# Attention scores: the pass over the keys' low part is cut to the 64 rows that hold the queries' high part, with two heads on the two row halves of TensorE

## The chip, the cores and the metric

The kernel runs on one core of a Trainium2 chip. The metric is the device time of one execution in microseconds, of which several runs are made; one execution was also taken by the hardware profiler, and all rows below come from that one. In the rows PE is TensorE's matmul, PEld its weight load, DVE is VectorE, ACT is ScalarE, POOL is GpSimd, SP is SyncE.

## The reference

Two layers of a diffusion backbone, over 128 context tokens and 512 latent tokens (five token tiles of 128). A layer has one input projection, a state-space branch, two attention branches with 8 heads of 64 (2 key heads, each shared by 4 query heads), a gated merge, and an MLP of width 4096. What the change touches is the score product of the two attention branches:

```
def _blocked_attention(q, k, v, sink):
...
        s = jnp.einsum('bqhgd,bkhd->bhgqk', qq, k).astype(jnp.float32) * ATTN_SCALE
...
        p = jax.nn.softmax(s, axis=-1)[..., :n_k]
        return jnp.einsum('bhgqk,bkhd->bqhgd', p.astype(v.dtype), v)
```

The windowed branch does the same over the key tiles within 128 positions, the 128 cached context keys and a sink logit; the global branch sees all 512 latent keys and the 128 cached ones. The context tile sees itself only.

## The kernel before

Every fp32 product is split: an operand is written as a high part (rounded to the shorter matmul type) and a low part (what is left), and a product is made of three passes (high by high, low by high, high by low) that accumulate in one PSUM bank.

The scores do this in two passes. `queries` (line 863) writes for each of the 8 heads a stationary operand `qs[:, hd]` of 128 rows by 128 queries. The 64 rows of a head's high part lie in the lower half (rows 0 to 63) for even heads and in the upper half (rows 64 to 127) for odd heads, and the low part is in the other half. `keys` (line 837) writes `KH` and `KL`, the keys' high and low part, each **twice**, in both row halves. So one pass of `KH` over 128 rows adds high by high and low by high at once (line 915), and one pass of `KL` adds high by low and low by low (line 916).

`attend` (line 876) takes one token tile: for each of 2 key heads `v` and 2 pairs of query heads `pr` it writes the scores of the pair into two banks `pp[0]` and `pp[1]` (tag `sc`, three such banks in all), one bank for each head. The key blocks are grouped into `runs` of neighbours, one matmul of 128 to 512 columns for each run. In the windowed branch (`i == 0`) a pass with `maskb` (line 920) adds the band's mask. In the global branch (`i == 1`) the last two key blocks go to a third bank `p5` (lines 923 to 925). Then VectorE takes the maxima (line 926), ScalarE the exponentials (line 938), TensorE transposes them (line 947), they are split (line 950) and multiplied with the values (lines 954 and 955).

The pair-of-heads loop runs 4 times in a token tile, 5 token tiles, 2 branches and 2 layers: 80 pairs, 160 heads. Attention is not alone on TensorE: the order in which each engine's instructions stand is made at build time by a scheduler with a timeline model, which places matmuls of the projections and gates (lines 159 to 161 and 170 to 172) between those of attention. Each engine then runs its instructions in that order, and waits on semaphores.

Some matmuls of the kernel use only part of TensorE's columns: the transposes of the keys by `ident` (line 855: 64 columns, two column halves) and the conditioning product (lines 187 and 524: 32 columns, four column groups). No matmul of the kernel before uses only part of the rows.

Of the kernel before, what the change touches and what calls it, by code (L numbers as in the profile page):

```python
# [30 lines left out]
def net(tc, I, O, depth=DEPTH, dbg=None):  # L31
    nc = tc.nc
    V, S, G, T, SY = nc.vector, nc.scalar, nc.gpsimd, nc.tensor, nc.sync
# [26 lines left out]
    def psc():  # L60
        return bank("sc", 3)

    def ppt():
        return bank("pt", 2)

    def ppv():
        return bank("pv", 1)
# [17 lines left out]
    identb = base.tile([128, 128], BF, name="identb")  # L85
    V.tensor_copy(identb, ident)
    maskb = base.tile([128, 384], BF, name="maskb")
# [29 lines left out]
    def split(hi, lo, src, half=False):  # L117

        if half:
            S.activation(hi, src, AF.Copy, scale=0.5)  # L120
            V.scalar_tensor_tensor(lo, src, 0.5, hi, op0=ALU.mult, op1=ALU.subtract)
        else:
            S.activation(hi, src, AF.Copy)  # L123
            V.tensor_tensor(lo, src, hi, op=ALU.subtract)  # L124
# [368 lines left out]
    def phase_a(l, h):  # L493
# [113 lines left out]
        for ft in range(4):  # L607
            ws = wtile(I["w_u"][l, ft], 8) if ft >= len(uacc) else None
            us = uall[:, ft]
            for c in (0, 17, 83):  # L610
                n = 2 if c == 17 else 1
                G.memset(us[:, :, c:c + n], 0.0)
            for i, (t0, t1) in enumerate(SPLITS):
                n = (t1 - t0) * 128
# [3 lines left out]
                v = p[:, :n].rearrange("p (c j) -> p j c", j=8)  # L618
# [257 lines left out]
        def attend(i, t, qs, KH, KL, VV, y):  # L876

            if t == 0:
                blks = (0,)
            elif i == 0:  # L880
                blks = tuple(b for b in (t - 1, t, t + 1) if 1 <= b <= 4) + (5,)
            else:
                blks = (1, 2, 3, 4, 5)

            runs = []
            n1 = 4 if len(blks) < 5 else 3
            for b in blks[:n1]:
                if runs and runs[-1][-1] == b - 1:
                    runs[-1].append(b)
                else:  # L890
                    runs.append([b])
            nb = len(blks)
            order = blks
            stat = atp[0].tile([128, 4, 8], F32, name="stat", tag="stat", bufs=2)
            ng, sm, sx, rs = (stat[:, j] for j in range(4))
            for v in range(2):
                po = ppv()
                for pr in range(2):
                    h0 = 4 * v + 2 * pr
                    hs = slice(h0, h0 + 2)  # L900
                    part = atp[0].tile([128, 2, 2], F32, name="part", tag="part", bufs=4)

                    pp = [psc(), psc()]
                    p5 = psc() if nb > 4 else None
                    n4 = 128 * min(nb, n1)
                    Ps = [atp[0].tile([128, 640 if i else 512], F32, name="P", tag="P", bufs=4) for _ in range(2)]
                    for z_ in range(2):
                        hd = h0 + z_
                        o = 0
                        for r in runs:  # L910
                            n = 128 * len(r)
                            c0 = 128 * r[0]
                            oo = pp[z_][:, o:o + n]
                            msk = i == 0 and t > 0 and r[0] < 5
                            T.matmul(oo, qs[:, hd], KH[:, v, c0:c0 + n], start=True, stop=False)
                            T.matmul(oo, qs[:, hd], KL[:, v, c0:c0 + n], start=False, stop=not msk)
                            if msk:
                                nm = 128 * sum(b < 5 for b in r)
                                m0 = 128 * (r[0] - t + 1)
                                T.matmul(oo[:, 0:nm], identb, maskb[:, m0:m0 + nm], start=False, stop=True)  # L920
                            o += n
                        if p5 is not None:
                            o5 = p5[:, 256 * z_:256 * z_ + 256]
                            T.matmul(o5, qs[:, hd], KH[:, v, 512:768], start=True, stop=False)
                            T.matmul(o5, qs[:, hd], KL[:, v, 512:768], start=False, stop=True)
                        V.reduce_max(part[:, 0, z_:z_ + 1], pp[z_][:, 0:n4], axis=AX.X, negate=True)
                    n0 = part[:, 0]
                    if i == 0:
                        V.tensor_tensor(ng[:, hs], n0, nsink[:, 1, hs], op=ALU.min)
                    else:  # L930
                        if p5 is not None:
                            V.reduce_max(part[:, 1], p5.rearrange("p (z n) -> p z n", z=2), axis=AX.X, negate=True)
                            V.tensor_tensor(n0, n0, part[:, 1], op=ALU.min)
                        V.tensor_tensor(ng[:, hs], n0, ssq[:, t, hs], op=ALU.mult)  # L934
                    for z_ in range(2):
                        oh = slice(h0 + z_, h0 + z_ + 1)
                        sc_ = ssq[:, t, oh] if i else 1.0
                        S.activation(Ps[z_][:, 0:n4], pp[z_][:, 0:n4], AF.Exp, scale=sc_, bias=ng[:, oh], accum_out=sm[:, oh])
                        if p5 is not None:
                            S.activation(Ps[z_][:, 384:640], p5[:, 256 * z_:256 * z_ + 256], AF.Exp, scale=sc_, bias=ng[:, oh], accum_out=sx[:, oh])  # L940
                    for z0 in range(0, nb, 2):
                        zs = range(z0, min(z0 + 2, nb))
                        n = 256 * len(zs)
                        p = ppt()
                        for z in zs:
                            for z_ in range(2):
                                T.transpose(p[:, (2 * (z - z0) + z_) * 128:(2 * (z - z0) + z_ + 1) * 128], Ps[z_][:, z * 128:(z + 1) * 128], ident)
                        ph = atp[0].tile([128, 512], F32R, name="ph", tag="ph", bufs=3)
                        pl = atp[0].tile([128, 512], F32R, name="pl", tag="pl", bufs=2)
                        split(ph[:, 0:n], pl[:, 0:n], p[:, 0:n])  # L950
                        for z in zs:
                            zc = slice(256 * (z - z0), 256 * (z - z0) + 256)
                            oo = po[:, 256 * pr:256 * pr + 256]
                            T.matmul(oo, VV[:, order[z], v], ph[:, zc], start=(z == 0), stop=False)
                            T.matmul(oo, VV[:, order[z], v], pl[:, zc], start=False, stop=(z == nb - 1))

                pz = po.rearrange("p (r z n) -> p r z n", r=2, z=2)
                yv = y[:, t, 2 * v:2 * v + 2]
                yt = atp[0].tile([128, 2, 128], F32, name="yt", tag="yt", bufs=2 if i else 1)
                S.activation(yt[0:64], pz[64:128, :, 0], AF.Copy)  # L960
                S.activation(yt[64:128], pz[0:64, :, 1], AF.Copy)
                V.tensor_tensor(yv[0:64], pz[0:64, :, 0], yt[0:64], op=ALU.add)
                V.tensor_tensor(yv[64:128], pz[64:128, :, 1], yt[64:128], op=ALU.add)
            if nb > 4:
                V.tensor_tensor(sm, sm, sx, op=ALU.add)
            if i == 0:
                V.tensor_tensor(sx, nsink[:, 0], ng, op=ALU.add)
                S.activation(sx, sx, AF.Exp)
                V.tensor_tensor(sm, sm, sx, op=ALU.add)
            V.reciprocal(rs, sm)  # L970

            rx = atp[0].tile([128, 640 if i else 512], F32, name="P", tag="P", bufs=4)[:, 0:512].rearrange("p (a b) -> p a b", a=8)
            S.activation(rx, rs.unsqueeze(2).to_broadcast([128, 8, 64]), AF.Copy)
            p = ppt()
            for j in range(4):
                T.transpose(p[:, j * 128:(j + 1) * 128], rx[:, 2 * j:2 * j + 2].rearrange("p a b -> p (a b)"), ident)
            V.tensor_tensor(y[:, t], y[:, t], p.rearrange("p (j n) -> p j n", j=4), op=ALU.mult)
# [8 lines left out]
        def attend_all(i, K, y):  # L986
            qs = qtile(i, 0)
            for t in range(NT):
                nxt = qtile(i, t + 1) if t + 1 < NT else None
                attend(i, t, qs, *K, y)  # L990
                qs = nxt
# [18 lines left out]
        for b in range(8):  # L1010
# [9 lines left out]
            for q in range(4):  # L1020
                o = p[:, q * NCH:(q + 1) * NCH]
# [100 lines left out]
        for i2 in range(2):  # L1122
            ws = wtile(I["w_glu"][l, i2], 4)
            for f in range(2):
                ft = 2 * i2 + f
                sg = t640("sg")
                for t0, t1 in SPLITS:
                    p = pg()
                    n = (t1 - t0) * 128
# [360 lines left out]
```

## Time and profile before

| | before |
|---|---|
| median of 3 runs | 2401.14 us (2400.68 to 2404.61) |
| the profiled execution | 2402.64 us |
| its span, first to last instruction | 2400.8 us |
| mean granted TensorE clock | 0.977 |
| PE busy / weight load busy | 95% / 86% of the span |
| DVE / ACT / POOL busy | 62% / 41% / 23% |

The profiled execution's own time lies 1.8 us around its span, and 1.5 us above the median. A matmul's row shows its start and a modelled length; matmuls overlap, so the pace of TensorE is read from one start to the next, not from the length. The form `128*64` in a row means 128 rows and 64 columns of TensorE, `128x384` that 384 columns stream.

### The profile page before, as it was taken

The page shows a single profiled execution, that of the slowest core. Times are in us where ns is not written, and L with a number is a line of the kernel's source. Part 1 is how long each engine was busy: PE and PEld are TensorE (multiplying, and loading weights), DVE is VectorE, ACT ScalarE, POOL GpSimd, SP SyncE. Part 2 cuts the span into 40 slices and gives each one's busy share as a digit, 9 for nine tenths or more (in the row PEclk, how much of TensorE's full clock was granted, in tenths as well). Part 3 has the DMA queues.
Part 4 walks back from the last instruction along what each step waited for, and adds up shares of the span by engine and source line. Part 5 has one row for each costly group of instructions (what it writes and reads, how often), then busy time and mean ns, then how long its engine had stood idle before and what let it go on. Part 6 is the DMA issues. An engine that isn't in the chain of part 4 may idle for free. (4 is left out here: it accounts for less than half of the span.)

```text
span 2400.8 us, 38820 instructions
## 1 busy us (share of the span) xinstructions
PE 2287.4 (95%) x14904; PEld 2072.1 (86%) x14904; DVE 1481.5 (62%) x3001; ACT 990.9 (41%) x2316; POOL 556.6 (23%) x615
## 2 busy tenths in 40 slices
PE   7887999999999999999998889999999889999997
PEld 4777897799997988888888889999999789998885
DVE  7887854766348956663665766466743873444457
ACT  2324655565344432222234256566642353332221
POOL 2555700001024311100531661000102550000046
PEclk8998999999999999999999999999999999999999
DMA  7423236722232345556335313522222422222221
GB/s 271 138 82 106 94 114 210 237 79 83 80 132 75 117 152 172 172 166 201 125 105 148 116 60 118 156 68 72 72 74 68 175 80 79 73 78 77 74 80 53
DMA packets 126361, 277.93 MB, mean 116 GB/s; under 512 B 40640, under 2 KB 60224, under 8 KB 126176
## 3 DMA queue, kind: packets, MB, share of 16 engines
q1 hardware_dynamic: 126176, 275.45, 35.2%
q8 instruction: 117, 1.92, 0.3%
q14 instruction: 68, 0.56, 0.1%
HBM read 240.97 MB, written 38.63 MB: 116 GB/s over the span
## 5 line engine op out<-in xcount | busy, mean ns | idle before, releaser
L124 DVE TENSOR_TENSOR wlo<-raw,whi 128x512 fp32r<-128x512 f32 x472 | 361.3, 773 | 296.1 <-ACT whi L123 288.9
L123 ACT ACTIVATE whi<-raw 128x512 fp32r<-128x512 f32 x472 | 292.6, 631 | 437.7 <-PE p_sc L1206 144.5
L159 PE MATMUL p_g<-hh,whi 128*128 128x256 f32 (+1 forms) x1224 | 384.5, 315 | 4.0 <-ACT hh L123 3.1
L161 PE MATMUL p_g<-hh,wlo 128*128 128x256 f32 (+1 forms) x1224 | 383.0, 314 | 3.5 <-DVE wlo L124 3.3
L160 PE MATMUL p_g<-hl,whi 128*128 128x256 f32 (+1 forms) x1224 | 382.7, 313 | 3.3 <-DVE hl L124 3.3
L159 PEld LDWEIGHTS p_g<-hh,whi 128*128 128x128 f32 x1224 | 234.0, 191 | 11.8 <-ACT hh L123 3.9
L161 PEld LDWEIGHTS p_g<-hh,wlo 128*128 128x128 f32 x1224 | 234.1, 191 | 5.6 <-DVE wlo L124 5.0
L160 PEld LDWEIGHTS p_g<-hl,whi 128*128 128x128 f32 x1224 | 234.4, 191 | 4.6 <-DVE hl L124 4.0
L159 PE MATMUL p_sc<-hh,whi 128*128 128x256 f32 (+1 forms) x648 | 203.2, 315 | 4.8 <-ACT hh L123 4.5
L160 PE MATMUL p_sc<-hl,whi 128*128 128x256 f32 (+1 forms) x648 | 203.3, 314 | 4.0 <-DVE hl L124 4.0
L161 PE MATMUL p_sc<-hh,wlo 128*128 128x256 f32 (+1 forms) x648 | 202.7, 313 | 0.1
L1090 POOL TENSOR_TENSOR mt<-sg,mt 128x640 f32<-128x640 f32 x24 | 40.5, 1686 | 647.5 <-DVE stat L934 276.4
L170 PE MATMUL p_g<-whi,hh 128*128 128x256 f32 x480 | 143.1, 301 | 10.0 <-DVE rt L785 6.2
L171 PE MATMUL p_g<-wlo,hh 128*128 128x256 f32 x480 | 142.3, 297 | 3.9 <-DVE wlo L124 3.4
L159 PE MATMUL p_g<-act,whi 128*128 128x384 f32 x448 | 141.3, 315 | 4.7 <-ACT mtmp L192 3.0
L124 DVE TENSOR_TENSOR pl<-p_pt,ph 128x512 fp32r<-128x512 f32 (+1 forms) x176 | 102.9, 591 | 64.0 <-ACT ph L123 54.1
L1290 DVE TENSOR_TENSOR rl<-rl 128x384 f32<-128x384 f32 (+1 forms) x128 | 75.9, 594 | 106.3 <-ACT rl L1289 106.3
L172 PE MATMUL p_g<-whi,hl 128*128 128x256 f32 x480 | 140.8, 294 | 0.0
L161 PE MATMUL p_g<-act,wlo 128*128 128x384 f32 x448 | 139.2, 311 | 0.0
L160 PE MATMUL p_g<-act,whi 128*128 128x384 f32 x448 | 138.7, 310 | 0.0
L159 PEld LDWEIGHTS p_sc<-hh,whi 128*128 128x128 f32 x648 | 124.6, 193 | 11.3 <-ACT hh L123 5.0
L1205 PE MATMUL p_sc<-wlo,ff 128*128 128x512 f32 x336 | 133.7, 398 | 0.0
(428 smaller groups left out, 5755.1 us busy)
## 6 DMA issues: line engine op xcount, KB each, us to landing
raw<-in_w_mod_dram SPq DMA_DIRECT2D x96, 512.0 KB
raw<-in_w_up_dram SPq DMA_DIRECT2D x64, 512.0 KB
raw<-in_w_down_dram SPq DMA_DIRECT2D x64, 512.0 KB
raw<-in_w_gate_dram SPq DMA_DIRECT2D x48, 512.0 KB
raw<-in_w_br_dram SPq DMA_DIRECT2D x24, 512.0 KB
raw<-in_w_q_dram SPq DMA_DIRECT2D x16, 512.0 KB
ctab_d<-prow SPq DMA_DIRECT2D x16, 512.0 KB
tab<-ctab_d SPq DMA_DIRECT2D x16, 512.0 KB
```

What stands on the lines that cost most here:

```text
L123: S.activation(hi, src, AF.Copy)
L124: V.tensor_tensor(lo, src, hi, op=ALU.subtract)
L159: T.matmul(out, wh, tok(ah, t0, t1), start=(first and k == 0), stop=False)
L160: T.matmul(out, wh, tok(al, t0, t1), start=False, stop=False)
L161: T.matmul(out, wl, tok(ah, t0, t1), start=False, stop=(last and k == n - 1))
L170: T.matmul(out, ah, wh, start=(first and k == 0), stop=False)
L171: T.matmul(out, ah, wl, start=False, stop=False)
L172: T.matmul(out, al, wh, start=False, stop=(last and k == n - 1))
L1090: G.tensor_tensor(mtv[:, ft], sg, mtv[:, ft], op=ALU.add)
L1205: T.matmul(banks[t], a_, wl, start=False, stop=False)
L1290: V.tensor_tensor(r[:, :n], r[:, :n], r[:, :n], op=ALU.mult)
```

## The change

The score loop is written in another order, and the `KL` pass is cut in half by rows. Per pair of heads: first all `KH` passes (and masks, and the unchanged `p5` passes of both heads), then the `KL` passes, which take only the 64 rows of the queries' high part (`zp`, rows 0 to 63 for the even head, 64 to 127 for the odd one), with the two heads next to each other in the code. The product low by low, which the 128-row pass added, is left out. The number of passes and their columns stay as they were. `start` is set on the first run of a bank only, since passes of all runs are now open in one bank together. The maxima are taken in a loop behind the passes.

```diff
-                            T.matmul(oo, qs[:, hd], KH[:, v, c0:c0 + n], start=True, stop=False)
-                            T.matmul(oo, qs[:, hd], KL[:, v, c0:c0 + n], start=False, stop=not msk)
+                            T.matmul(oo, qs[:, hd], KH[:, v, c0:c0 + n], start=(o == 0), stop=False)
                             if msk:
...
-                                T.matmul(oo[:, 0:nm], identb, maskb[:, m0:m0 + nm], start=False, stop=True)
+                                T.matmul(oo[:, 0:nm], identb, maskb[:, m0:m0 + nm], start=False, stop=False)
...
+                    o = 0
+                    for r in runs:
+                        n = 128 * len(r)
+                        c0 = 128 * r[0]
+                        for z_ in range(2):
+                            zp = slice(64 * z_, 64 * z_ + 64)
+                            T.matmul(pp[z_][:, o:o + n], qs[zp, h0 + z_], KL[zp, v, c0:c0 + n], start=False, stop=(r is runs[-1]))
+                        o += n
+                    for z_ in range(2):
                         V.reduce_max(part[:, 0, z_:z_ + 1], pp[z_][:, 0:n4], axis=AX.X, negate=True)
```

The order that the scheduler then makes is shown at three places. In the changed kernel the `KL` pass is line 931, the mask 919, the `p5` passes 922 and 923, the transposes of the exponentials 955 and the value passes 962 and 963 (before: 916, 920, 924 and 925, 947, 954 and 955). The numbers behind `p_sc` tell the banks' tiles apart: one number is one head.

TensorE, layer 0, windowed branch, the first pair of token tile 2: heads 2836 and 2837, before.

```order
L915 MATMUL p_sc_2836<-KH_2440,qs_2620 128x384
L916 MATMUL p_sc_2836<-KL_2441,qs_2620 128x384
L920 LDWEIGHTS identb_70
L920 MATMUL p_sc_2836<-maskb_72,identb_70 128x384
L915 MATMUL p_sc_2836<-KH_2440,qs_2620 128x128
L916 MATMUL p_sc_2836<-KL_2441,qs_2620 128x128
L955 MATMUL p_pv_2631<-pl_2711,VV_2442 128x256
...
L915 MATMUL p_sc_2837<-KH_2440,qs_2620 128x384
L916 MATMUL p_sc_2837<-KL_2441,qs_2620 128x384
```

The same place in the changed kernel.

```order
L915 MATMUL p_sc_2836<-KH_2440,qs_2620 128x384
L919 LDWEIGHTS identb_70
L919 MATMUL p_sc_2836<-maskb_72,identb_70 128x384
L915 MATMUL p_sc_2836<-KH_2440,qs_2620 128x128
L931 MATMUL p_sc_2836<-KL_2441,qs_2620 128x384
L931 MATMUL p_sc_2836<-KL_2441,qs_2620 128x128
L963 MATMUL p_pv_2631<-pl_2711,VV_2442 128x256
...
L915 MATMUL p_sc_2837<-KH_2440,qs_2620 128x384
...
L931 MATMUL p_sc_2837<-KL_2441,qs_2620 128x384
L931 MATMUL p_sc_2837<-KL_2441,qs_2620 128x128
```

The two `KL` passes of one head moved behind its `KH` passes and its mask and stand side by side; those of the other head come 32 rows later, behind 24 projection matmuls and others.

TensorE, layer 0, global branch, the first pair of token tile 1: heads 4670 and 4671 and their shared bank 4672, in the changed kernel (before, the rows are the same with the lines of before).

```order
L915 MATMUL p_sc_4670<-KH_4473,qs_4531 128x384
L931 MATMUL p_sc_4670<-KL_4474,qs_4531 128x384
L955 MATMUL p_pt_4632<-ident_63,P_4621 128x128
L922 MATMUL p_sc_4672<-KH_4473,qs_4531 128x256
L923 MATMUL p_sc_4672<-KL_4474,qs_4531 128x256
L922 MATMUL p_sc_4672<-KH_4473,qs_4531 128x256
L923 MATMUL p_sc_4672<-KL_4474,qs_4531 128x256
L955 MATMUL p_pt_4632<-ident_63,P_4622 128x128
L915 MATMUL p_sc_4671<-KH_4473,qs_4531 128x384
L931 MATMUL p_sc_4671<-KL_4474,qs_4531 128x384
L962 MATMUL p_pv_4594<-ph_4612,VV_4475 128x256
```

Nothing moved here: each head's `KL` pass still follows its own `KH` pass, and full-width passes stand between the two heads.

TensorE, layer 1, windowed branch, the context tile: heads 15036 and 15037 in the changed kernel.

```order
L172 MATMUL p_g_14754<-whi_14637,hl1_13280 128x256
L915 MATMUL p_sc_15036<-KH_14970,qs_15013 128x128
L915 MATMUL p_sc_15037<-KH_14970,qs_15013 128x128
L931 MATMUL p_sc_15036<-KL_14971,qs_15013 128x128
L931 MATMUL p_sc_15037<-KL_14971,qs_15013 128x128
L915 MATMUL p_sc_15059<-KH_14970,qs_15013 128x128
```

Here the second head's `KH` pass moved ahead of the first head's `KL` pass, and the `KL` passes of two heads stand next to each other. That is so at two places of the program, this one and one in the context tile of layer 1's global branch.

## Rows read from the trace of the kernel before

**Rows 1.** The page, part 1: busy us, share of the span, instructions.
```profile
PE 2287.4 (95%) x14904; PEld 2072.1 (86%) x14904; DVE 1481.5 (62%) x3001; ACT 990.9 (41%) x2316; POOL 556.6 (23%) x615
```

**Rows 2.** Busy time of each engine in the four stretches with score passes.
```profile
core 0: us, PE busy (x) PEld busy (x) DVE busy (x) ACT busy (x) POOL busy (x), PEclk, DMA share, GB/s
214.00:356.00 142.00, 133.43 (x965) 125.82 (x966) 102.86 (x202) 84.39 (x265) 67.39 (x127) 0.97 0.28 92
392.00:573.00 181.00, 175.61 (x1226) 152.79 (x1225) 127.01 (x269) 114.49 (x278) 4.69 (x3) 0.99 0.48 164
1383.00:1531.00 148.00, 140.80 (x1057) 134.05 (x1057) 96.47 (x206) 87.46 (x295) 43.87 (x84) 0.98 0.32 99
1567.00:1742.00 175.00, 174.11 (x1264) 173.06 (x1263) 121.92 (x254) 113.38 (x283) 8.21 (x5) 1.00 0.22 72
```

**Rows 3.** Groups by line and form, the KL passes: count, busy us, mean ns.
```profile
L916 PE MATMUL p_sc<-KL,qs 128*128 128x384 f32 x96 | 32.8, 342 | 0.0
...
L916 PE MATMUL p_sc<-KL,qs 128*128 128x128 f32 x64 | 17.4, 282 | 0.0
...
L916 PE MATMUL p_sc<-KL,qs 128*128 128x512 f32 x16 | 6.3, 394 | 0.0
...
L916 PE MATMUL p_sc<-KL,qs 128*128 128x256 f32 x16 | 4.5, 280 | 0.0
```

**Rows 4.** Timeline of PE at a head's two score passes: start us, length us.
```profile
1604.45 0.34 PE L915 MATMUL p_sc<-KH,qs 128*128 128x384 f32 x1
1604.63 0.34 PE L916 MATMUL p_sc<-KL,qs 128*128 128x384 f32 x1
1604.80 0.28 PE L955 MATMUL p_pv<-pl,VV 128*128 128x256 f32 x1
```

**Rows 5.** Timeline of PE around two matmuls on 64 of its columns.
```profile
1357.66 0.28 PE L171 MATMUL p_g<-wlo,hh 128*128 128x256 f32 x1
1357.78 0.28 PE L172 MATMUL p_g<-whi,hl 128*128 128x256 f32 x1
1357.99 0.43 PE L855 MATMUL p_pt<-ident,kf 128*64 128x128 f32 x2
1358.36 0.38 PE L170 MATMUL p_g<-whi,hh 128*128 128x256 f32 x1
1358.58 0.28 PE L171 MATMUL p_g<-wlo,hh 128*128 128x256 f32 x1
```

**Rows 6.** Timeline of PEld, the weight loads at the end of that place.
```profile
1358.35 0.19 PEld L170 LDWEIGHTS p_g<-whi,hh 128*128 128x128 f32 x1 [0.17 <-issue]
1358.46 0.19 PEld L171 LDWEIGHTS p_g<-wlo,hh 128*128 128x128 f32 x1
```

**Rows 7.** Timeline of PE: one full-width matmul between two 64-column groups.
```profile
1362.67 0.27 PE L855 MATMUL p_pt<-ident,kf 128*64 128x128 f32 x1
1362.68 0.27 PE L855 MATMUL p_pt<-ident,P 128*64 128x128 f32 x1
1362.88 0.38 PE L170 MATMUL p_g<-whi,hh 128*128 128x256 f32 x1
1363.19 0.43 PE L855 MATMUL p_pt<-ident,P 128*64 128x128 f32 x2
1363.56 0.39 PE L171 MATMUL p_g<-wlo,hh 128*128 128x256 f32 x1
1363.78 0.28 PE L172 MATMUL p_g<-whi,hl 128*128 128x256 f32 x1
```

**Rows 8.** Waits of PE in 214 to 356 us: total, times, longest.
```profile
PE p_g L170 <- DVE rt L785: 3.7, 2, 3.0
PE p_g L161 <- DVE wlo L124: 1.9, 1, 1.9
```

**Rows 9.** Waits of PE in 1383 to 1531 us.
```profile
PE p_g L170 <- DVE rt L785: 2.5, 1, 2.5
PE p_pv L955 <- DVE pl L124: 2.5, 2, 1.4
```

More of the change, by code (lines that the diff above doesn't have):

```diff
@@ L919, in attend @@
                                 m0 = 128 * (r[0] - t + 1)
-                                T.matmul(oo[:, 0:nm], identb, maskb[:, m0:m0 + nm], start=False, stop=True)
+                                T.matmul(oo[:, 0:nm], identb, maskb[:, m0:m0 + nm], start=False, stop=False)
                             o += n
                         if p5 is not None:
-                            o5 = p5[:, 256 * z_:256 * z_ + 256]
-                            T.matmul(o5, qs[:, hd], KH[:, v, 512:768], start=True, stop=False)
-                            T.matmul(o5, qs[:, hd], KL[:, v, 512:768], start=False, stop=True)
+                            T.matmul(p5[:, 256 * z_:256 * z_ + 256], qs[:, hd], KH[:, v, 512:768], start=True, stop=False)
+                            T.matmul(p5[:, 256 * z_:256 * z_ + 256], qs[:, hd], KL[:, v, 512:768], start=False, stop=True)
+                    o = 0
[7 more added lines that the diff above has]
+                    for z_ in range(2):
                         V.reduce_max(part[:, 0, z_:z_ + 1], pp[z_][:, 0:n4], axis=AX.X, negate=True)
```

## Prediction

> **What bounds the kernel now.** I read the page first. TensorE is busy 95% of the span, VectorE 62%, the rest less [rows 1], so a microsecond more or less on TensorE should reach the end, unless it falls into a stretch where TensorE waits anyway. The score passes lie in four stretches, so I looked at those alone [rows 2]: the windowed branch (142 and 148 us) and the global branch (181 and 175 us) of the two layers. TensorE's idle time in them is what the stretch is longer than its busy time: 8.6, 5.4, 7.2 and 0.9 us, 22.1 us of 646. The granted clock is 0.97 to 1.00 there, so it runs at the upper level (2.4 GHz) nearly throughout. The waits that make up the idle time are few and long: 3.7 us for the queries' rotation, 1.9 us for a weight's low part [rows 8], 2.5 us each for two others [rows 9]. In these stretches TensorE is therefore the bound, its program order is fixed at build time, and the change is to be costed as time on TensorE.
>
> **What the change does to the passes.** There are 192 KL passes: 96 of 384 columns, 64 of 128, 16 of 512, 16 of 256 [rows 3], that is 57,344 columns. A pass of 384 columns takes 0.17 us from its start to the next start, and so does the KH pass ahead of it [rows 4]. At that pace all KL passes are 57,344 / 384 x 0.17 = 25 us. Their number and columns stay, only the rows are halved. No matmul of the kernel before uses part of the rows, so what a lone 64-row pass takes is not shown. From below it could take half (12.7 us less in all), from above twice as long (25 us more, if row halves stream at half the pace); I take the same time, because the pace seen goes by columns: 0.17 us for 384 [rows 4], 0.12 for 256 [rows 5], and columns stay. A saving then needs the partner: if the two heads of a pair ran at the same time, half of the 25 us, 12.7 us, would go. That two parts of TensorE can run together is seen on column halves: two 64-column matmuls start 0.01 us apart [rows 7].
>
> But the order of the changed kernel, shown above, does not put the partners together. The bank of a pair's second head becomes free late, and the scheduler puts the first head's KL passes right behind that head's KH passes, as before. I counted all of it: the 192 passes stand in 159 groups without anything between, and only two of these groups hold more than one head (both in a context tile, with 128-column passes). 30 of the others hold two runs of the same head, which use the same row half. So the saving is that of two pairs of 128 columns, below 0.2 us in all. **Term 1: 0.**
>
> **What it adds: 159 visits to another mode.** Each group is entered from full-width work and left for it. What a change of the used part of TensorE costs is not shown for rows. It is shown for columns. In steady work a 256-column matmul starts 0.12 us after the one ahead (1357.66 to 1357.78) [rows 5]. The last one before the 64-column group is followed after 0.21 us (1357.78 to 1357.99), and the first one behind the group is itself followed after 0.22 us (1358.36 to 1358.58) instead of 0.12 [rows 5]. So a change costs about 0.09 us ahead of it and 0.10 us behind it. The second part has its reason in the weight loads: in steady work a load starts some 0.12 us ahead of its matmul (L171: load 1358.46 [rows 6], matmul 1358.58 [rows 5]), while the first matmul behind the change starts together with its load (L170: 1358.35 [rows 6] and 1358.36 [rows 5]); the load is not hidden. A full-width matmul that stands alone between two such groups pays both parts: 0.31 us to the next start (1362.88 to 1363.19) instead of 0.12 [rows 7], 0.19 more for one change behind its start and one ahead of it. A visit, one change in and one out, therefore costs 2 x 0.19 = 0.38 us.
>
> The Trainium skill, TensorEngine Tiling (Array Packing), Key Properties, says that a change of the tiling mode, not of the tile alone, drains TensorE, and counts halves by rows among the modes. The column rows above agree with it (0.09 us lost before the change); for rows nothing here shows it. By this rule the price above holds for row halves too; without it the sum below would be near 0.
>
> Count of changes: 159 visits make 318; 7 visits are followed at once by a 32-column conditioning product, where one change was paid already, so 311. **Term 2: 311 x 0.19 = 59.1 us.** Bounds of the price: from below 0 (row halves may be entered without a stop), from above 0.22 us (a two-matmul group between full-width work: 1357.78 to 1358.58 is 0.80 us [rows 5], where three steady 256-column starts take 0.36, so 0.44 for two changes), that is 0 to 68 us. I take 0.19, because the group of one or two matmuls between full-width ones is the same situation, and the price seen comes from the array running empty and an unhidden load, neither of which speaks of columns in particular.
>
> **What of it is hidden.** Where TensorE waited for something that does not hang on its own last passes, it now arrives later and waits less. There are 22.1 us of such idle time at most [rows 2]; much of it ends with VectorE work on matmuls of the same stretch (the rotation, the split of the exponentials) [rows 8, 9], which is late by the same amount. I take a third: **term 3: -7 us**, bounds 0 and -22.
>
> **What else moves.** The mask now stands ahead of KL; it costs the same. A head's maximum still waits for its KL passes, as before; it comes 0.2 to 0.3 us later, and the exponentials and transposes behind it too, while TensorE has other matmuls between. `start` on the first run alone adds no instruction. No transfer is added; the transfers of weights have more time. In layer 1 the scheduler shuffles some projection matmuls between the heads; I put that at 0, within 5 us either way, less than the 8.1 us that TensorE idles in layer 1's two stretches [rows 2].
>
> **Sum**, against the profiled execution's 2402.64 us: 2402.6 + 0 + 59.1 - 7 = 2454.7 us. The median lies 1.5 us below that execution, so I predict 2453 us, 2.2% slower. On this kernel 0.2%, about 4.8 us, is what a measurement can tell from no change.
>
> **The rivals.**
> - *Entering a row half costs only the unhidden load* (0.10 us a change), not the empty array: 311 x 0.10 = 31 us, some 5 hidden, about 2426 us. For it: of the two parts seen, only the load's has a reason that must hold for rows as well. Against: the array's part was there at both ends of every column group shown.
> - *The mode change is free*, and the change does nothing, since the pairs that it writes don't stand together in the program: 2401 us, within 0.2%. For it: row halves were never seen; a weight load for a part of the rows could be placed beside running work. Against: rows 5 to 7.
> - *Faster*: the change is free and the shuffled order in layer 1 recovers waits. At most the 8.1 us of layer 1's idle time, so 2393 us or above. It decides only if a change costs below 8.1 / 311 = 0.03 us, a seventh of what columns show.
> - *The heads run side by side after all.* The Trainium skill, TensorE: Matmul & The Clock Gate, Why this matters for your kernels, gives this as the gain of short contractions: slices in different row groups run concurrently, and one alone takes as long as a full one. The second half agrees with the count above. Worked out from rows, as if all 80 pairs stood together: 12.7 us saved, 160 changes at 0.19, 30 us lost, so 18 us slower still, 2420 us; a pair would gain only below 12.7 / 160 = 0.08 us a change. The order excludes it at all but two places, so it has no chance of its own.
>
> **How the numbers follow.** The full price as on columns, with 0 to 22 us hidden and up to 0.22 us a change (2438 to 2470 us): 0.70. Half the price or the load alone (about 2415 to 2438): 0.16. Free, no difference: 0.09. Faster: 0.05. The predicted time is the first case's, and its own range 2438 to 2470. The range for 8 in 10 reaches down into the second case and up to the upper price, with 2 us for the shuffled order: 2420 to 2472. Slower by over 0.2%: 0.70 + 0.16 = 0.86; within 0.2%: 0.09; faster: 0.05.
>
> **What the profile after would show.** KL rows at line 931 with 64 rows and the same lengths as before in columns; a start-to-start time of about 0.37 us for a lone 384-column KL pass instead of 0.17, about 0.09 us more ahead of it and 0.10 more behind the matmul that follows; weight loads of KL that start with their matmul instead of ahead of it. The two windowed stretches longer by 10 to 16 us each and the global ones by 13 to 16, everything else of equal length; VectorE's and ScalarE's busy time as before. Wrong would be: KL passes of two heads that start together in more than two places; lone KL passes at 0.17 us (price 0); a KL pass whose streaming itself takes longer on half the rows, which would add up to the 25 us above; or a stretch outside the four that changes by more than 5 us.

## The result, and the profile after

| | before | after |
|---|---|---|
| median | 2402.88 us (2400.68 to 2406.07, 4 runs) | 2445.18 us (2445.07 to 2446.77, 4 runs) |
| the profiled execution, and its span | 2402.64, 2400.8 us | 2445.19, 2443.4 us |

The changed kernel is slower: the ratio of after to before is 1.0175, 95% interval 1.0159 to 1.0191, so 42.3 us more. The forecast was 2453 us, 52 us more than the median that was known then, with a range of 2420 to 2472.

The page of the changed kernel, part 1, answers to [rows 1]: busy us, share of the span, instructions.

```profile
PE 2339.2 (96%) x14904; PEld 2083.0 (85%) x14904; DVE 1485.6 (61%) x3001; ACT 994.4 (41%) x2316; POOL 556.7 (23%) x615
```

TensorE's busy time grew by 51.8 us with the same 14,904 matmuls; VectorE's and ScalarE's grew by about 4 us. The four stretches with score passes (bounds moved along with the work) answer to [rows 2].

```profile
core 0: us, PE busy (x) PEld busy (x) DVE busy (x) ACT busy (x) POOL busy (x), PEclk, DMA share, GB/s
212.00:361.00 149.00, 144.80 (x965) 129.13 (x966) 103.66 (x202) 84.97 (x265) 67.50 (x128) 0.97 0.29 88
397.00:590.00 193.00, 189.04 (x1234) 154.75 (x1232) 129.63 (x271) 116.17 (x281) 5.07 (x3) 0.99 0.47 155
1399.00:1558.00 159.00, 153.47 (x1055) 137.78 (x1054) 98.97 (x208) 87.53 (x292) 45.36 (x86) 0.98 0.30 92
1598.00:1787.00 189.00, 188.75 (x1272) 175.06 (x1272) 122.87 (x256) 116.58 (x285) 8.56 (x5) 1.00 0.22 67
```

They are 690 us long instead of 646: 7, 12, 11 and 14 us more. That is 44 us with bounds in whole us, where the span grew by 42.6 us, so the whole difference lies in them. The granted clock is what it was (0.97 to 1.00), so no part of it is the clock. TensorE's idle time in them (length less busy time) fell from 22.1 to 13.9 us.

The groups of KL passes by line and form answer to [rows 3]: `64*128` says 64 rows and 128 columns of TensorE.

```profile
L931 PE MATMUL p_sc<-KL,qs 64*128 64x384 f32 x96 | 42.0, 438 | 0.0
...
L931 PE MATMUL p_sc<-KL,qs 64*128 64x128 f32 x64 | 17.1, 280 | 0.0
L931 PE MATMUL p_sc<-KL,qs 64*128 64x512 f32 x16 | 8.0, 497 | 0.0
...
L931 PE MATMUL p_sc<-KL,qs 64*128 64x256 f32 x16 | 6.3, 392 | 0.0
```

A 384-column pass has become 96 ns longer (342 before), a 512-column one 103 ns, a 256-column one 112 ns. The mean of the 128-column ones did not move (282 and 280 ns), because about half of them now stand behind another KL pass in the same visit and are shorter for it. Why the others are longer is seen in the timelines of PE and of PEld at one head of layer 1's global branch (start us, length us), the counterpart of [rows 4].

```profile
1645.77 0.27 PE L955 MATMUL p_pt<-ident,P 128*128 128x128 f32 x1
1645.79 0.42 PE L915 MATMUL p_sc<-KH,qs 128*128 128x384 f32 x1
1646.15 0.43 PE L931 MATMUL p_sc<-KL,qs 64*128 64x384 f32 x1
1646.51 0.39 PE L159 MATMUL p_g<-act,whi 128*128 128x256 f32 x1
1646.73 0.28 PE L160 MATMUL p_g<-act,whi 128*128 128x256 f32 x1
1646.85 0.28 PE L161 MATMUL p_g<-act,wlo 128*128 128x256 f32 x1
```

```profile
1646.15 0.18 PEld L931 LDWEIGHTS p_sc<-KL,qs 64*128 64x128 f32 x1 [0.19 <-issue]
1646.51 0.19 PEld L159 LDWEIGHTS p_g<-act,whi 128*128 128x128 f32 x1 [0.18 <-DVE mt L1096]
1646.62 0.19 PEld L160 LDWEIGHTS p_g<-act,whi 128*128 128x128 f32 x1
```

The lone KL pass takes 0.36 us to the next start (1646.15 to 1646.51) instead of 0.17. Its weight load starts with it, at 1646.15, and so does that of the matmul behind it, at 1646.51, which itself takes 0.22 us instead of 0.12. In steady work the load is 0.11 us ahead (L160: 1646.62 and 1646.73). The KH pass ahead of it takes 0.36 us, of which only 0.10 belongs to the visit: it stands right behind a transpose (L955), and there a 384-column KH pass took 0.26 us before as well. Over all 384-column KH passes ahead of a visit the medians are 0.27 us, where it was 0.18, and behind a transpose 0.35, where it was 0.26. This is the picture of the column groups in [rows 5 to 7], at the same price: 0.09 us ahead of each change, read as the array running empty, and 0.10 us of unhidden load behind it. The two parts are read from the rows; no run takes one away without the other.

Another reading of the longer KL rows is that 64 rows stream at a slower pace. The starts of all matmuls of the trace exclude it. A lone visit's one pass of 256, 384 or 512 columns takes 0.31, 0.37 or 0.43 us to the next start, where full-width passes take 0.12, 0.17 and 0.23: 0.19 or 0.20 us more whatever the columns. (The 256 columns stand alone once here and 65 times in the kernel with two visits below, with the same time; a lone 128-column pass takes 0.25, 0.14 more.) At half the pace the addition would have grown from 0.12 to 0.23 us.

### The profile page after: what moved, and what is told of

The parts are those of the page before. It is cut to its first block, busy times and chain, and to the rows that moved or that the text cites. A ratio compares the mean times of both kernels' runs of the same rounds, so it can differ in the third digit from the quotient of the medians.

```text
span 2443.4 us, 38811 instructions
## 1 busy us (share of the span) xinstructions
PE 2339.2 (96%) x14904; PEld 2083.0 (85%) x14904; DVE 1485.6 (61%) x3001; ACT 994.4 (41%) x2316; POOL 556.7 (23%) x615
## 4 chain that ended last, share of the span: by engine, by line
PE 80%; DVE 9%; POOL 4%; DMA 3%; issue 2%; ACT 2%; SPq 1%; DVEq 0%; ACTq 0%; POOLq 0%
PE p_g L159 9%; PE p_g L160 9%; PE p_g L161 9%; PE p_sc L159 4%; PE p_sc L160 4%; PE p_sc L161 4%; PE p_sc L1212 4%; PE p_sc L1213 4%; PE p_sc L1214 3%; PE p_pt L955 3%; PE p_g L1212 2%; PE p_g L1213 2%; PE p_g L1214 2%; PE p_sc L931 2%; PE p_g L1033 2%
## 5 line engine op out<-in xcount | busy, mean ns | idle before, releaser
L160 PE MATMUL p_g<-hl,whi 128*128 128x256 f32 (+1 forms) x1224 | 384.1, 314 | 2.5 <-DVE hl L124 2.5
L160 PEld LDWEIGHTS p_g<-hl,whi 128*128 128x128 f32 x1224 | 234.2, 191 | 7.8 <-issue 4.1
L160 PE MATMUL p_sc<-hl,whi 128*128 128x256 f32 (+1 forms) x648 | 203.8, 315 | 3.9 <-DVE hl L124 3.9
L160 PE MATMUL p_g<-act,whi 128*128 128x384 f32 x448 | 139.7, 312 | 0.0
```

What stands on the lines that cost most here:

```text
L160: T.matmul(out, wh, tok(al, t0, t1), start=False, stop=False)
```

## The experiments

Six kernels were run, each timed against the kernel before on the same chip.

**KL on all 128 rows, in the changed order.** It tells the row halves apart from everything else that the change does.

```diff
-                            T.matmul(pp[z_][:, o:o + n], qs[zp, h0 + z_], KL[zp, v, c0:c0 + n], start=False, stop=(r is runs[-1]))
+                            T.matmul(pp[z_][:, o:o + n], qs[:, h0 + z_], KL[:, v, c0:c0 + n], start=False, stop=(r is runs[-1]))
```

> The changed kernel with its KL pass on all 128 rows again (the low-by-low product is back), the code order of the change kept. Theory 'mode changes' (the added time is what TensorE loses on entering and leaving row halves): no visits to row halves are left, so the time of the kernel before, 2403 us, within 5 us. Rival 'order' (the new order of passes and maxima, and the projections shuffled in layer 1, cost the time): about 2445 us, as the changed kernel.

Measured: 2405.29 us, ratio 1.0005 (0.9995 to 1.0015). In its trace TensorE's 14,904 matmuls start in the same order as in the changed kernel, so the two kernels differ in the rows alone. The order of passes, masks and maxima, and the shuffled projections, cost nothing that can be measured (at most 0.15%); the added time comes from the row halves. The rival of the order falls.

**The row halves in one branch only.** In the code of the change, the other branch gets the full rows; the windowed branch alone is shown, for the global one the condition is `i == 1`.

```diff
-                            zp = slice(64 * z_, 64 * z_ + 64)
+                            zp = slice(64 * z_, 64 * z_ + 64) if i == 0 else slice(0, 128)
```

> The changed kernel with 64 rows in the windowed branch only; the global branch's KL passes use 128 rows. Theory 'mode changes': only the two windowed stretches grow, by 7 and 11 us as in the changed kernel (80 visits at 0.38 is 30 us, much of it in waits there): about 2421 us. Rival 'order': 2445 us.

> The changed kernel with 64 rows in the global branch only; the windowed branch's KL passes use 128 rows. Theory 'mode changes': only the two global stretches grow, by 11 and 14 us as in the changed kernel (79 visits at 0.38 is 30 us, little of it hidden): about 2428 us; the growth of this kernel and of the one with the windowed branch alone add up to that of the changed kernel, 42 us, within 5. Rival 'order': 2445 us.

Measured: 2421.09 us, ratio 1.0068 (1.0047 to 1.0088), and 2430.00 us, ratio 1.0114 (1.0088 to 1.0139). The two parts, 0.68% and 1.14%, add up to 1.82%, where both together are 1.75%. About the same number of visits (81 and 78) seems to cost less in the windowed branch than in the global one, though the two intervals meet at 1.0088. That idle time is the reason is not shown, but it fits: in the changed kernel the stretch with the most idle time before (8.6 us) grew least, by 7 us, and the one with the least (0.9 us) grew most, by 14 [rows 2].

**Partners held together.** The KL passes of a pair are put behind the KH passes of both its heads, in the scheduler's order only.

```diff
-                            T.matmul(oo, qs[:, hd], KH[:, v, c0:c0 + n], start=(o == 0), stop=False)
+                            kh = T.matmul(oo, qs[:, hd], KH[:, v, c0:c0 + n], start=(o == 0), stop=False)
...
-                    for r in runs:
+                    with tc.issue_after(kh.ins):
+                        for r in runs:
...
```

> The changed kernel with the KL passes of both heads held back until both heads' KH passes are issued, so that partners do stand together: 90 visits instead of 159, 74 of them with two heads. Theory 'mode changes': 182 more changes than with full rows at 0.19 us is 35 us, less 11 to 12 us for passes that run side by side, less some 6 hidden: about 2420 us, still slower than before; with waits for the second head's bank up to 2440. In the trace partners start within 0.02 us of each other and a visit still costs 0.4 us. Rival 'the pairing was all that was missing': 2403 less 12 is about 2391 us. Rival 'row halves do not run side by side': partners start 0.17 us apart for 384 columns, and the time is 2430 us or above.

Measured: 2417.78 us, ratio 1.0058 (1.0037 to 1.0079). This is what the change says it does, and it is still slower than before, by 14 us. Its timeline of PE, at a pair of layer 1's global branch:

```profile
1615.27 0.34 PE L915 MATMUL p_sc<-KH,qs 128*128 128x384 f32 x1
1615.54 0.45 PE L932 MATMUL p_sc<-KL,qs 64*128 64x384 f32 x2
1615.91 0.39 PE L160 MATMUL p_g<-act,whi 128*128 128x256 f32 x1
1616.13 0.28 PE L161 MATMUL p_g<-act,wlo 128*128 128x256 f32 x1
```

Two KL passes of 384 columns, in one row of the timeline (x2), are over after 0.37 us, as the lone one was after 0.36: the partner is free, the row halves do run side by side. But the visit's price is unchanged (0.27 us ahead of it instead of 0.17, 0.22 behind it instead of 0.12). The rivals "pairing was all that was missing" and "no side by side" both fall. The held order was not run on full rows, but the traces say where the loss is: summed as in term 2 below, over the whole program, the excess next to and in the KL passes is 20.9 us, against 7.1 in the kernel with full rows, and the waits of over 0.3 us elsewhere are no longer than there (111.4 and 112.2 us).

**Two visits for a head.** In the global branch's latent tiles the KL pass is cut in two visits (256 and 128 columns) with full-width passes held between, once on row halves and once, in the same order instruction by instruction, on full rows.

```diff
+                            zp = slice(64 * z_, 64 * z_ + 64)
+                            ka = T.matmul(pp[z_][:, 0:256], qs[zp, hd], KL[zp, v, 128:384], start=False, stop=False)
+                            with tc.issue_after(ka.ins):
                                 T.matmul(p5[:, 256 * z_:256 * z_ + 256], qs[:, hd], KH[:, v, 512:768], start=True, stop=False)
-                            T.matmul(p5[:, 256 * z_:256 * z_ + 256], qs[:, hd], KL[:, v, 512:768], start=False, stop=True)
+                                kb = T.matmul(p5[:, 256 * z_:256 * z_ + 256], qs[:, hd], KL[:, v, 512:768], start=False, stop=True)
+                            with tc.issue_after(kb.ins):
+                                T.matmul(pp[z_][:, 256:384], qs[zp, hd], KL[zp, v, 384:512], start=False, stop=True)
...
-                    for r in runs:
+                    for r in (runs if p5 is None else []):
```

> The changed kernel with each head's KL pass of the global branch's latent tiles cut into two visits to its 64 rows (256 and 128 columns), with full-width passes of the last two key blocks held between them: 222 visits instead of 159, 435 mode changes more than with full rows. Theory 'mode changes, a quarter hidden': 435 x 0.19 is 83 us, some 16 hidden, 67 us over the same order with full rows, so about 2474 us, 29 us over the changed kernel. Rival 'the loss comes once a head, not with every visit': as the changed kernel plus the same order's extra passes, about 2450 us.

> The same order of instructions as the kernel with two visits a head, with all its KL passes on 128 rows: no visits to row halves. Theory 'mode changes': only the 64 extra passes cost, 0.06 us each, 4 us: about 2407 us. Rival 'cutting the pass and the held order cost the time': 2430 us or above.

Measured: 2479.18 us, ratio 1.0300 (1.0271 to 1.0329), and 2413.63 us, ratio 1.0038 (1.0025 to 1.0051). The difference of the two is 65.6 us, where 67 were expected (the first one's interval alone is 7 us either way): the loss comes with every visit, not once a head. The control was 7 us above its expectation: its held order makes TensorE wait more (start-to-start times of over 0.3 us beyond the steady ones add up to 32.9 us in its four stretches, 27.0 in the kernel before), which the expectation had left out.

## Why the prediction was right, step by step

**The bound.** TensorE's time in the four stretches reached the end, and no stretch outside of them moved by more than 3 us. As said. The shares of the stretches came out less well: 7 us in the first windowed one, where 10 to 16 were forecast, and 12 in the first global one, where 13 to 16 were; more was hidden there than term 3 allowed.

**Term 1, nothing saved.** Right: KL passes of two heads stand together at two places, and what is saved there is some 0.2 us. With full rows in the same order the time is that of before, and with partners held together 14 us are lost instead of 42.

**Term 2, 59.1 us for mode changes.** The mechanism is shown, by the rows above, by the kernel with full rows in the same order and by the two kernels with two visits. For its size I added up, over all matmuls of the four stretches, what each start-to-start time exceeds the steady one for its columns (0.11, 0.12, 0.17 and 0.23 us for 128, 256, 384 and 512). Next to and in the KL passes this excess is 4.2 us before and 60.2 us after: 56.0 us, for 307 more mode changes in the program's order, 0.18 us each. (The prediction's 311 is the difference to full rows in the same order, which has four changes fewer than the kernel before; against that kernel's trace the sum is 53.5 us, 0.17 each. Other choices of the steady times move these differences by about 1 us.) That the price of column groups is the price of row halves too was a bet, since no row of the kernel before showed it; it came out, so the rivals "unhidden load only" (0.10) and "free" fall. The Trainium skill's rule in TensorEngine Tiling (Array Packing), Key Properties, is that a change of mode drains TensorE. The trace agrees with it for row halves: the row ahead of the KL pass is stretched by 0.09 us.

**Term 3, 7 us hidden.** This is the step that was mis-sized. In the same sum the excesses of over 0.3 us elsewhere (waits) fell from 27.0 to 17.5 us, and the small ones from 5.4 to 1.1: 13.8 us were hidden, twice the term. 56.0 - 13.8 = 42.2 us, where the two profiled executions differ by 42.55. I had taken a third of 22.1 us of idle time; but idle time in the stretches is counted from the modelled ends of matmuls, which lie 0.16 us behind the pace, so it misses a part of each wait and all short ones. The stock was 27.0 + 5.4 = 32 us, and some 40% of it went (against the kernel with full rows in the same order, 11 us of 32). Waits for weights and for split exponentials shrank most, as the waits of PE in the two windowed stretches after tell (212 to 361 us, then 1399 to 1558 us: total, times, longest), against [rows 8, 9] and one more row of before (1383 to 1531 us), which stands first:

```profile
PE p_g L161 <- DVE wlo L124: 1.1, 1, 1.1
```

```profile
PE p_g L170 <- DVE rt L785: 3.2, 2, 2.6
...
PE p_g L161 <- DVE wlo L124: 0.3, 1, 0.3
```

```profile
PE p_g L170 <- DVE rt L785: 3.2, 1, 3.2
PE p_g L171 <- DVE wlo L124: 1.1, 1, 1.1
PE p_pv L962 <- ACT ph L123: 0.8, 3, 0.3
PE p_pv L963 <- DVE pl L124: 0.3, 1, 0.3
```

The waits for the queries' rotation, which hangs on TensorE's own last passes, stayed (6.2 us before, 6.4 after). Those for the weights' low part fell from 1.9 to 0.3 in layer 0 and stayed at 1.1 in layer 1 (before at line 161, after at line 171). That for the exponentials' low part fell from 2.5 to 0.3 (the one for their high part rose from 0.4 to 0.8). So the prediction was right that the wait for the rotation hides nothing, but it counted the split of the exponentials there too, and that wait nearly went; too little was put on the side that hides.

**The rival "side by side"** was worked out as 2420 us, 18 us slower, for 80 pairs that all stand together. The kernel that holds most of them together took 2417.78 us. That the two are so close is in part luck: that kernel has 74 pairs together and 182 more changes, not 80 and 160. The sum's 25 us for all KL passes also priced 128-column passes by their columns, at 0.06 us; they run at 0.11, which makes it 29 us, and the saving of the partners 14.5 us instead of 12.7.

No version came out ahead of the kernel before. A visit costs 0.36 to 0.39 us; a partner saves one head's passes, at most 0.28 us (384 and 128 columns) in this kernel. A visit would have to hold the passes of two pairs or more, for which the three score banks have no room by the count of banks (one for each head); that was not tried.

## What to carry to other kernels

Before cutting a matmul to a part of TensorE's rows or columns, count the visits in the program's final order, not in the code: here each cost 0.36 to 0.39 us between full-width matmuls, more than a 512-column pass (0.23 us). By these numbers row halves would pay only where the partners really stand together and a visit holds enough columns to save more than that; no run here shows such a case. Where a kernel already has groups on part of the columns, as this one did, their rows in its trace show what to expect. And for what such a loss can hide behind, count TensorE's waits from start to start, since its busy time covers part of them.

## What was not expected

A weight load for 64 rows takes as long as one for 128 (0.18 and 0.19 us above), so half the rows save nothing there either. And a KL pass that stands second in a visit, on the same row half, pays little: 0.15 us for 128 columns, against 0.25 where such a pass stands alone. What costs is the visit, not the pass.
